# Two pairs of gate tiles by seven block products, softmax's small operations in pairs, one subtraction on GpSimd, four outputs begun early

## The chip, the cores and the metric

The kernel runs on one core of one Trainium2 chip. The metric is the time of one execution on the device, in microseconds; lower is better. Each kernel is run several times and the median is compared.

## The reference, cut to what matters

One decoder layer in float32, with 1024 tokens and 1024 channels:

```python
h = rms_norm(x, norm_mix_pre)
q_d, k_d, v_d, u_p, q_m, gate_logits = split(h @ w_in)
# branch A: 8 heads, two softmax maps per head, 64 wide; values 128 wide
s = q @ k * 64 ** -0.5 - slope[head] * distance          # causal
p = softmax(s)
a = (p[0] - lam * p[1]) @ v
y_attn = (rms_norm(a, subln_g) * 0.8) @ w_attn_branch
y_pool, y_mem = ...                                       # branches B and C
gates = sigmoid(gate_logits)                              # three times 1024 channels
mix = gates[0] * y_attn + gates[1] * y_pool + gates[2] * y_mem
x = x + rms_norm(mix @ w_out, norm_mix_post)
... gated feed-forward layer with a convolution over three tokens
```

The change touches the first gate's logits (gates[0], 1024 channels), the attention's softmax, the norm of each head and the product with `w_attn_branch`.

## The kernel before, in words

Activations lie transposed, channels on the 128 partitions and tokens along the free axis. A "tile" of a projection is 128 output channels by 1024 tokens. Every float32 operand is split into a high half (a copy to a type with fewer bits, on ScalarE) and a low half (the difference, on VectorE), and each product is three matmuls: high by high, high by low, low by high (`mm3`, lines 103 to 105; `split`, lines 89 and 90). The gate logits are thus, tile by tile, either

- `gate(dt)` (line 1116): one tile, 2 token halves x 8 channel blocks x 3 matmuls of 128x512 = 48 matmuls. It is a generator of eight steps of 6 matmuls each, so that it can be dealt out between other work; or
- `channels(c0)` with `seven` (line 198): two tiles at once as a 2 x 2 block product by seven products of half size (a Strassen-Winograd form with sums of weights and of inputs), each product 4 blocks x 3 matmuls, together 84 matmuls. The sums of inputs (`hops`, T1 to T4) exist only in the stage ahead of the attention.

The stages around the change are, in order:

1. The channel stage (to about 606 us of the span). `channels` makes the gates of the two other branches, keys of heads 0 and 1, all queries (four pairs of tiles, stored to `q_d` by SP) and gate tiles 0 and 1.
2. The attention, 8 heads of 4 blocks of 2 x 128 queries (606 to 882 us). Per block: `scores` (line 1161 on TensorE, the bias and the running maximum in one VectorE instruction at 1165, the exponent with its sum on ScalarE at 1170), `combine` for each of the two query tiles (reciprocal 1181, a small product 1182, and the difference of the two maps 1184, all on VectorE), `turn_weights` (transposes, line 1200, then a split), `weigh_values` (line 1217, then copy, square, and the square's two halves, 1219 to 1226), and `head_norm` (a product with ones, line 1235, whose row goes to `ss_d` by GpSimd's DMA queue). The first tile's `combine` is called right after the second tile's scores; the second tile's one block later, ahead of the turn. Between these stages `weave` deals out fillers: projections of the next head's keys (heads 1 to 6), and the gate tiles that `GATES` names: tiles 2 and 3 in head 0, tile 4 in head 7.
3. After the last weighing: `turn_sums(1)`, `load_norms(1)`, then gate tiles 5, 6 and 7, the norms of heads 4 to 7 (`head_norms(1)`, VectorE, written to `r_d` by SP and read back as a row for all partitions), and per head a load of its output `a`, of its row `rb`, a product (line 1384) and a split into `ath` and `atl`.
4. The merge: `merge_heads(dt, g)` adds the product of `w_attn_branch` with the heads of group g (0 to 3, 4 to 7) for output tile dt, `merge(dt)` applies the gate, adds the other two branches and splits. Outputs 0 and 1 are begun with group 0 ahead of heads 4 to 7.

Each engine takes its instructions in an order fixed when the program is built: a planner goes by the order of the program, lets an engine that would stand idle take a later instruction that is ready, and `issue_after(x)` holds the instructions of its block behind x on x's engine. SP and GpSimd issue the DMAs, in such an order too. Tile pools of one side are stacked: a pool that is closed hands its place to the next one, and a new tile waits for the last users of the tiles that lay there. The attention's pools are, in order, `qkp` (queries and keys), `att` and `vp` (values); `atp` (`ath`, `atl`) and `sub` (`a`, `rb`) take their place.

Of the kernel before, what the change touches and what calls it, by code (L numbers as in the profile page):

```python
# [8 lines left out]
F32 = mybir.dt.float32  # L9
# [3 lines left out]
ALU = mybir.AluOpType  # L13
# [28 lines left out]
def kernel(  # L42
# [818 lines left out]
    with tc.tile_pool(name="gp", reuse_waits="tile", bufs=2, side="right") as gp_:  # L861
# [163 lines left out]

        ss = gp_.tile([P, 4, H4, P], F32, tag="g", name="ss", bufs=3)
# [4 lines left out]
        ready = {2: wsplit(chunk(w_in, C_G + 2 * P), [P, KT, P])}  # L1031
        with tc.issue_after(ready[2][2].ins):
            late[0]()
# [10 lines left out]
    bias = ap_.tile([P, 1152], F32, name="bias", bufs=1)  # L1044
# [5 lines left out]
    def head_bias(h):  # L1050
        biases[h] = ap_.tile([P, 1152], F32, tag="hbias", name="hbias", bufs=2)
        nc.scalar.activation(out=biases[h], in_=bias, func=AF.Copy, scale=2.0 ** -(h + 1))
# [87 lines left out]
    def scores(h, b, u):  # L1140
# [9 lines left out]
        sm = small.tile([P, 1], F32, tag="sm", name="sm")  # L1150
# [5 lines left out]
        for c in range(2):  # L1156
            pss = bank2(name="pss2")
            for i in range(parts):
                keys = ks[c][:, i * m:(i + 1) * m]
                for j in range(2):  # L1160
                    last["scores"] = nc.tensor.matmul(pss[:, i * H:i * H + m], q[:, j, c, ts], keys,  # L1161
                                                      start=(j == 0), stop=(j == 1))
            z = ap_.tile([P, S], F32, tag="z%d" % c, name="z", bufs=3 - c)
# [7 lines left out]
                                 bias=mx[:, c:c + 1], accum_out=sm if c else sums[:, h, t:t + 1])  # L1171
        exps[h, b, u] = z2, mx, sm
# [3 lines left out]
    def combine(h, b, u):  # L1176

        z2, mx, sm = exps.pop((h, b, u))
        t = 2 * b + u
        n = (t + 1) * P  # L1180
        nc.vector.reciprocal(out=mx[:, 1:2], in_=sm)
        nc.vector.scalar_tensor_tensor(
            out=mx[:, 0:1], in0=mx[:, 1:2], scalar=sums[:, h, t:t + 1], in1=nlam, op0=ALU.mult, op1=ALU.mult)
        last["combine"] = nc.vector.scalar_tensor_tensor(
            out=z2[0][:, 0:n], in0=z2[1][:, 0:n], scalar=mx[:, 0:1], in1=z2[0][:, 0:n],
            op0=ALU.mult, op1=ALU.add)
        zts[h, b, u] = z2[0]
# [17 lines left out]
    def weigh_values(h, b):  # L1205
# [10 lines left out]
        for n, ((k, qs, w, ws), i, j) in enumerate(terms):  # L1216
            nc.tensor.matmul(po[:, qs], (vh, vl)[i][:, k, :], w[j][:, ws], start=(n == 0), stop=(n == len(terms) - 1))  # L1217
# [580 lines left out]
```

## Time and profile before

| | before |
|---|---|
| time, median of 3 runs | 1728.39 us (1727.39 to 1730.04) |
| profiled execution, span from first to last instruction | 1727.6 us |
| mean granted clock of TensorE | 0.999 |
| busy: ScalarE | 886.6 us (51%) |
| busy: GpSimd | 45.0 us (3%) |
| DMA traffic | 294.41 MB, mean 170 GB/s |

The page gives no time of the profiled execution other than its span. Busy time of an engine is the union of its instructions. PE is TensorE, PEld its weight loads (beside the matmuls), DVE VectorE, ACT ScalarE, POOL GpSimd, SP the queue that issues most DMAs. The ends of matmuls are modelled: each 128x512 matmul is shown as about 390 ns although the next one starts after some 226 ns, so the starts are to be read. A window's row gives, behind its length, the busy time and the number of instructions of each engine.

### The profile page before, as it was taken

To read this page: it belongs to the slowest core of one execution; us is meant where nothing else is said; L and a number is where in the kernel's file an instruction comes from. 1 tells how busy PE (TensorE), PEld (TensorE's weight loads), DVE (VectorE), ACT (ScalarE), POOL (GpSimd) and SP (SyncE) were. 2 spreads that over 40 slices of the span, in tenths; PEclk is the share of its full clock that TensorE was granted. 3 is DMA by queue.
4 is the path that set the end of the run, shared out by engine and by line. 5 is a ranking of instruction groups with operands and counts; after the bars stand their busy time and mean duration, and the time that the engine had idled before them with its cause. 6 is when DMAs were issued, how large, how long until landed. Compare 5 with 4: busy or idle time off the path is not lost.

```text
span 1727.6 us, 22400 instructions
## 1 busy us (share of the span) xinstructions
PE 1712.8 (99%) x8106; PEld 1421.4 (82%) x8106; DVE 1241.3 (72%) x2047; ACT 886.6 (51%) x1577; POOL 45.0 (3%) x103
## 2 busy tenths in 40 slices
PE   9999999999999999999999999999999999999998
PEld 7888888887888888888888888888888888888886
DVE  6765875666665578888866555848888888878466
ACT  5434544434544467777754344645555555543453
POOL 0000000000000011111110000000000000000000
PEclk9999999999999999999999999999999999999999
DMA  8873544444874686665556571572333423583344
GB/s 273 317 281 114 163 150 133 166 147 143 266 237 159 201 231 170 176 182 152 145 187 239 176 230 50 171 225 92 124 112 107 122 85 98 190 299 106 107 149 142
DMA packets 232803, 294.41 MB, mean 170 GB/s; under 512 B 15865, under 2 KB 161526, under 8 KB 230006
## 3 DMA queue, kind: packets, MB, share of 16 engines
q1 hardware_dynamic: 229158, 285.61, 51.8%
q0 software_dynamic: 3520, 7.38, 1.2%
q8 instruction: 64, 1.05, 0.3%
q14 instruction: 45, 0.37, 0.1%
q10 hardware_dynamic: 16, 0.00, 0.0%
HBM read 201.10 MB, written 85.56 MB: 166 GB/s over the span
## 4 chain that ended last, share of the span: by engine, by line
PE 91%; DVE 5%; DMA 2%; ACT 1%; issue 1%; SPq 0%; DVEq 0%; ACTq 0%
PE pa L103 8%; PE pa L104 8%; PE pa L105 8%; PE pb L103 5%; PE pb L104 5%; PE pb L105 5%; PE pss L1161 3%; PE poa L1217 2%; PE pd L103 2%; PE pd L105 2%; PE pd L104 2%; PE pe L105 2%; PE pe L104 2%; PE pe L103 2%; PE pout L103 2%; PE pout L105 2%
## 5 line engine op out<-in xcount | busy, mean ns | idle before, releaser
L89 ACT ACTIVATE wpage<-s 128x512 fp32r<-128x512 f32 x136 | 85.3, 627 | 108.2 <-DVE s L188 35.3
L90 DVE TENSOR_TENSOR wpage<-s,wpage 128x512 fp32r<-128x512 f32 x136 | 92.8, 688 | 43.2 <-ACT wpage L89 43.2
L1565 DVE SCALAR_TENSOR_TENSOR cvt<-gv,cols,cvt 128x1023 f32<-128x1023 f32 x88 | 112.5, 1278 | 15.6 <-ACT cvt L1561 14.9
L1165 DVE CUSTOM_DVE_ANT_0 z<-pss,hbias 128x256 f32<-128x256 f32 (+7 forms) x128 | 94.5, 752 | 26.0 <-PE pss L1161 24.8
L1170 ACT ACTIVATE z<-z,mx 128x256 f32<-128x256 f32 (+7 forms) x128 | 98.8, 773 | 20.8 <-DVE mx L1165 20.7
L103 PE MATMUL pa<-T,wpage 128*128 128x512 f32 x264 | 102.8, 389 | 0.0
L105 PE MATMUL pa<-T,wpage 128*128 128x512 f32 x264 | 102.7, 389 | 0.0
L104 PE MATMUL pa<-T,wpage 128*128 128x512 f32 x264 | 102.7, 389 | 0.0
L1161 PE MATMUL pss<-ks,q 128*128 128x512 f32 (+5 forms) x384 | 86.6, 349 | 1.4 <-DVE mx L1165 1.4
L89 ACT ACTIVATE page<-blk 128x1024 fp32r<-128x1024 f32 (+1 forms) x42 | 41.4, 989 | 85.7 <-PE pe L104 50.6
L90 DVE TENSOR_TENSOR page<-blk,page 128x1024 fp32r<-128x1024 f32 (+1 forms) x42 | 47.5, 1130 | 38.1 <-ACT page L89 38.1
L1161 PEld LDWEIGHTS pss<-ks,q 128*128 128x128 f32 x384 | 62.9, 189 | 11.1 <-DVE mx L1165 6.2
L103 PE MATMUL pd<-page 128*128 128x512 f32 x176 | 68.7, 390 | 0.0
L104 PE MATMUL pd<-page 128*128 128x512 f32 x176 | 68.5, 389 | 0.0
L105 PE MATMUL pd<-page 128*128 128x512 f32 x176 | 68.3, 389 | 0.0
L103 PE MATMUL pa<-hT,wpage 128*128 128x512 f32 x168 | 65.5, 390 | 0.1
L105 PE MATMUL pa<-hT,wpage 128*128 128x512 f32 x168 | 65.4, 389 | 0.0
L104 PE MATMUL pa<-hT,wpage 128*128 128x512 f32 x168 | 65.4, 389 | 0.0
L1217 PEld LDWEIGHTS poa<-aT,v 128*128 128x128 f32 x480 | 60.7, 190 | 3.0 <-ACT srow L1237 1.4
L1217 PE MATMUL poa<-aT,v 128*128 128x256 f32 (+1 forms) x480 | 62.5, 280 | 0.0
L103 PEld LDWEIGHTS pa<-T,wpage 128*128 128x128 f32 x264 | 49.6, 188 | 10.7 <-DVE gv L250 0.3
L104 PEld LDWEIGHTS pa<-T,wpage 128*128 128x128 f32 x264 | 49.6, 188 | 10.2
(429 smaller groups left out, 4965.7 us busy)
## 6 DMA issues: line engine op xcount, KB each, us to landing
q<-q_d SPq DMA_DIRECT2D x64, 256.0 KB, 5.1
wd<-in_w_down_dram SPq DMA_DIRECT2D x22, 512.0 KB, 5.0
tw_d<-wd SPq DMA_DIRECT2D x11, 1024.0 KB
rawv<-in_w_up_dram SPq DMA_DIRECT2D x22, 512.0 KB, 5.8
rawu<-in_w_up_dram SPq DMA_DIRECT2D x22, 512.0 KB, 4.1
ff_d<-cvt SPq DMA_DIRECT2D x22, 512.0 KB, 5.4
blk<-ff_d SPq DMA_DIRECT2D x20, 512.0 KB, 7.9
br<-tw_d SPq DMA_DIRECT2D x20, 512.0 KB, 5.0
```

The source lines that it names most:

```text
L89: copy = nc.scalar.activation(out=hi, in_=src, func=AF.Copy)
L90: nc.vector.tensor_tensor(out=lo, in0=src, in1=hi.bitcast(F32), op=ALU.subtract)
L103: nc.tensor.matmul(o, ah, bh, start=first, stop=False, skip_group_check=onto)
L104: nc.tensor.matmul(o, ah, bl, start=False, stop=False, skip_group_check=onto)
L105: return nc.tensor.matmul(o, al, bh, start=False, stop=last, skip_group_check=onto)
L1161: last["scores"] = nc.tensor.matmul(pss[:, i * H:i * H + m], q[:, j, c, ts], keys, start=(j == 0), stop=(j == 1))
L1165: nc.vector.tensor_tensor_reduce(out=halves(z[:, 0:n]), in0=pss.rearrange("p (a m) -> p a m", a=2)[:, 0:parts, 0:m], in1=halves(biases[h][ ...
L1170: nc.scalar.activation(out=z[:, 0:n], in_=z[:, 0:n], func=AF.Exp, scale=-1.0, bias=mx[:, c:c + 1], accum_out=sm if c else sums[:, h, t:t + 1])
L1217: nc.tensor.matmul(po[:, qs], (vh, vl)[i][:, k, :], w[j][:, ws], start=(n == 0), stop=(n == len(terms) - 1))
L1565: nc.vector.scalar_tensor_tensor(out=cv[:, sh:], in0=u[:, 0:S - sh], scalar=w, in1=cv[:, sh:], op0=ALU.mult, op1=ALU.add)
```

## The change

- Gate tiles 2 to 5 are made in the channel stage, as two pairs by `channels`, and stored by SP. Head 0 keeps one gate tile as filler (now tile 6), head 7 gets the first four of tile 7's eight steps, and the other four come after the last block: the first of them free, three held behind the last weighing (`ends["poa"]`). Tile 4 is no longer in head 7, tiles 5 to 7 no longer after the attention.
- `combine` takes both query tiles of a block at once: one reciprocal and one small product over two columns, then the two differences. It is called one block later, ahead of the turn. The second map's tiles get three buffers instead of two.
- The low half of the squares is subtracted on GpSimd instead of VectorE, and the store of the head's output on GpSimd's queue stands behind it.
- The attention's pools change order (`vp`, `att`, `qkp`); the bias shares the buffers of the heads' biases, each made from the one before.
- The loads of heads 0 to 3 (`load_head`) come first after the attention, ahead of the norms' loads; their products and splits (`normed_head`) follow. The stores of the sums go by ScalarE's queue.
- The merge takes outputs in pairs, with weights in blocks of 4 x 256 columns; two pairs, outputs 0 to 3, are begun with heads 0 to 3, in all eight PSUM banks.

```diff
+        for dt in (2, 4):
+            g = channels(C_G + dt * P)
+            nc.sync.dma_start(out=gate_d[dt:dt + 2].rearrange("e p s -> p e s"), in_=g)
...
-        ready = {2: wsplit(chunk(w_in, C_G + 2 * P), [P, KT, P])}
+        ready = {6: wsplit(chunk(w_in, C_G + 6 * P), [P, KT, P])}
...
+    vpool = cstack.enter_context(tc.tile_pool(name="vp", reuse_waits="tile", bufs=2, side="right"))
+    ap_ = cstack.enter_context(tc.tile_pool(name="att", reuse_waits="tile", bufs=3, side="right"))
     qkp = cstack.enter_context(tc.tile_pool(name="qkp", reuse_waits="tile", bufs=1, side="right"))
-    ap_ = cstack.enter_context(tc.tile_pool(name="att", reuse_waits="tile", bufs=3, side="right"))
-    vpool = cstack.enter_context(tc.tile_pool(name="vp", reuse_waits="tile", bufs=2, side="right"))
...
-            z = ap_.tile([P, S], F32, tag="z%d" % c, name="z", bufs=3 - c)
+            z = ap_.tile([P, S], F32, tag="z%d" % c, name="z", bufs=3)
...
+    def combine(h, b):
+
+        both, sm = exps.pop((h, b))
+        nc.vector.reciprocal(out=sm, in_=sm)
         nc.vector.scalar_tensor_tensor(
-            out=mx[:, 0:1], in0=mx[:, 1:2], scalar=sums[:, h, t:t + 1], in1=nlam, op0=ALU.mult, op1=ALU.mult)
...
+            out=sm, in0=sm, scalar=nlam, in1=sums[:, h, 2 * b:2 * b + 2], op0=ALU.mult, op1=ALU.mult)
+        for u, (z0, z1) in enumerate(both):
+            n = (2 * b + u + 1) * P
+            last["combine"] = nc.vector.scalar_tensor_tensor(
+                out=z0[:, 0:n], in0=z1[:, 0:n], scalar=sm[:, u:u + 1], in1=z0[:, 0:n],
+                op0=ALU.mult, op1=ALU.add)
+            zts[h, b, u] = z0
...
-        nc.gpsimd.dma_start(out=ao_d[h][:, bs], in_=ao)
-
...
-        ends["square"] = nc.vector.tensor_tensor(out=sqs[1], in0=sq, in1=sqs[0].bitcast(F32), op=ALU.subtract)
+        ends["square"] = nc.gpsimd.tensor_tensor(out=sqs[1], in0=sq, in1=sqs[0].bitcast(F32), op=ALU.subtract)
+        nc.gpsimd.dma_start(out=ao_d[h][:, bs], in_=ao)
...
-        nc.sync.dma_start(out=sum_d[g * HG:(g + 1) * HG].rearrange("h (t p) -> (h t) p", p=P), in_=row)
+        nc.scalar.dma_start(out=sum_d[g * HG:(g + 1) * HG].rearrange("h (t p) -> (h t) p", p=P), in_=row)
...
-    GATES = ((2, 3), (), (), (), (), (), (), (4,))
...
-                    combine(*blocks[n - 1], 1)
+                    combine(*blocks[n - 1])
                     turn_weights(*blocks[n - 1])
                 stages.append(weights)
             stages.append(lambda h=h, b=b: scores(h, b, 1))
-            stages.append(lambda h=h, b=b: combine(h, b, 0))
...
+        if h == 0:
+            for n, step in enumerate(steps(first, 6)):
+                fillers.insert(min(2 * n, len(fillers)), step)
+        if h == NH - 1:
+            tail = steps(gate(7), 8)
+            fillers, tail = fillers + tail[:4], tail[4:]
...
-    def merge_heads(dt, g):
+    def merge_heads(d, g):
         if g == 0:
-            pys[dt] = wsplit(chunk(w_attn_branch, dt * P), [P, KT, P])[:2] + (bank(name="pya"), pbank(name="pya"))
...
+            both = ([bank2((P, 2, H), "pya") for _ in range(2)] if d % 2 == 0 else
+                    [(bank(name="pya"), pbank(name="pya")) for _ in range(2)])
+            pys[d] = [[b[:, 0, :], b[:, 1, :]] if d % 2 == 0 else list(b) for b in both]
+        wh, wl = mws.pop((d, g))
+        order = [(k, e, i) for k in range(H4) for e in range(2) for i in range(2)]
+        if d >= 2 and g == 1:
+            order = [(k, e, i) for e in range(2) for i in range(2) for k in range(H4)]
+        for k, e, i in order:
+            h, hs, es = g * HG + k, slice(i * H, (i + 1) * H), slice(e * P, (e + 1) * P)
+            mm3(pys[d][e][i], wh[:, k, es], wl[:, k, es], ath[h][:, hs], atl[h][:, hs], h == 0, h == NH - 1)
...
+        for h in range(HG):
+            load_head(h)
+        load_norms(1)
+        for n, step in enumerate(tail):
+            with tc.issue_after(ends["poa"].ins) if n else nullcontext():
+                step()
+        for h in range(HG):
+            normed_head(h)
+        merge_weights(1, 0)
+        with tc.issue_after(ends["square"].ins):
+            head_norms(1)
+        merge_heads(0, 0)
+        merge_weights(0, 1)
+        merge_heads(1, 0)
+        merge_weights(1, 1)
+        for h in range(HG, NH):
+            load_head(h)
+            normed_head(h)
```

More of the change, by code (lines that the diff above doesn't have):

```diff
@@ L1149, in scores @@
         mx = small.tile([P, 2], F32, tag="mx", name="mx")
-        sm = small.tile([P, 1], F32, tag="sm", name="sm")
+        if u == 0:
+            exps[h, b] = [], small.tile([P, 2], F32, tag="sm", name="sm")
+        both, sm = exps[h, b]
         z2 = []
@@ L1254, in load_norms @@
         for src, r in ((ss_d, 0), (sum_d, 3)):
[L1255 removed]
+            with tc.issue_after(marks["head"].ins) if g else nullcontext():
+                nc.sync.dma_start(out=st[:, r], in_=src[g * HG:(g + 1) * HG].rearrange("h (p f) -> p h f", f=8))
         hns[g] = st
@@ L1276 @@
     load_keys(0)
-    first = gate(2)
+    first = gate(6)
     head_bias(0)
@@ L1369, with load_head @@
                                 op0=ALU.mult)
-        for dt in range(5, KT):
-            for step in steps(gate(dt), 8):
-                step()
-        for h in range(NH):
-            if h == HG:
-                with tc.issue_after(ends["square"].ins):
-                    head_norms(1)
-                for dt in range(2):
-                    merge_heads(dt, 0)
+        heads = {}
+        def load_head(h):
             a = sub.tile([P, S], F32, tag="a", name="a")
```

69 lines of the change are left out of this document (30 added, 39 removed).

## The prediction

> **What bounds the kernel.** I read the page first (busy shares, granted clock), then busy time by windows cut at the stages around the change, then the waits of TensorE, then groups and timelines inside the attention.
>
> ```profile
> span 1727.6 us, 22400 instructions
> ...
> PE 1712.8 (99%) x8106; PEld 1421.4 (82%) x8106; DVE 1241.3 (72%) x2047; ACT 886.6 (51%) x1577; POOL 45.0 (3%) x103
> ```
>
> TensorE is busy for 99% of the span, so the question about every edit is what it does to TensorE's queue: fewer matmuls, or a hole in it. The windows are 40 us of the channel stage, head 0, head 4, head 7 up to its last scores, the last block's chain, the gate tiles after the attention, and the merge:
>
> ```profile
> 520.00:560.00 40.00, 40.00 (x179) 33.10 (x178) 22.80 (x32) 16.76 (x26) 0.00 (x0) 1.00 0.46 164
> ...
> 606.00:641.00 35.00, 34.24 (x186) 29.44 (x187) 25.81 (x66) 22.88 (x54) 4.46 (x8) 1.00 0.80 214
> ...
> 740.00:773.00 33.00, 32.62 (x203) 28.13 (x202) 28.97 (x76) 25.82 (x66) 4.33 (x9) 1.00 0.64 177
> ...
> 838.00:867.00 29.00, 27.83 (x168) 23.80 (x167) 24.13 (x63) 21.91 (x55) 4.30 (x8) 1.00 0.40 112
> 867.00:882.00 15.00, 15.00 (x97) 12.54 (x95) 10.16 (x18) 8.78 (x19) 2.12 (x4) 1.00 0.23 65
> 882.00:911.00 29.00, 29.00 (x129) 23.80 (x128) 16.78 (x29) 11.20 (x16) 3.78 (x7) 1.00 0.81 288
> 911.00:1000.00 89.00, 89.00 (x394) 73.68 (x394) 52.06 (x65) 37.20 (x50) 0.54 (x1) 1.00 0.63 209
> ```
>
> The columns are length, then busy us and count of PE, PEld, DVE, ACT, POOL, then clock, DMA share and GB/s. In the merge 394 matmuls fill 89.00 us: one 128x512 matmul costs 89.00/394 = 0.226 us of TensorE's queue, and the clock is full everywhere. Channel stage and merge have no hole; the heads have small ones, and in head 4 VectorE is busy 28.97 of 33 us, so it is the engine next in line. TensorE's waits between 600 and 940 us:
>
> ```profile
> PE pss L1161 <- DVE mx L1165: 1.4, 4, 0.5
> PE pta L1200 <- DVE z L1184: 1.3, 3, 0.6
> ...
> ```
>
> Together 2.7 us for VectorE in 340 us, none longer than 0.6. (A matmul's end is modelled later than the next one's start, so waits under some 0.2 us do not show.)
>
> **Step 1, the matmuls.** A gate tile alone takes 2 halves x 8 blocks x 3 = 48 matmuls of 512 columns, so tiles 2 to 5 take 192. As two pairs by seven products of 4 x 3 matmuls they take 2 x 84 = 168. 24 fewer: 24 x 0.226 = **-5.4 us**. The 168 go to the channel stage, where 179 matmuls fill 40 us already and VectorE is busy 22.80 of 40; that stage has another such pair of tiles every 19 us, with two 512 KB loads and a 1 MB store on SP's queue. I cost the move itself at nothing: the store of a pair waits on SP for the pair's last copy, ahead of the next pair's loads, just as the stores of the q channels do today, and TensorE shows no hole there.
>
> **Step 2, head 0.** It loses tile 3.
>
> ```profile
> L103 PE MATMUL pg<-hTh,wh 128*128 128x512 f32 x27 | 10.9, 403 | 0.6 <-ACT g L1130 0.6
> ```
>
> That is one of three like rows of this head: 81 gate matmuls, 18.3 us, fill it. Without 48 of them TensorE's work is 35.0 - 10.8 = 24.2 us. VectorE's is 25.8 us less what the change takes off it, which needs these rows (606 to 882 us):
>
> ```profile
> L1182 DVE SCALAR_TENSOR_TENSOR mx<-mx,sums,nlam 128x1 f32<-128x1 f32 x64 | 13.8, 215 | 4.8 <-ACT z L1170 3.7
> L1226 DVE TENSOR_TENSOR sq<-sq,sq 128x256 fp32r<-128x256 f32 x31 | 13.0, 420 | 2.4 <-ACT sq L1225 2.3
> ...
> L1181 DVE RECIPROCAL mx<-sm 128x1 f32<-128x1 f32 x64 | 10.0, 158 | 8.7 <-ACT z L1170 8.4
> ```
>
> One pair of small operations for two tiles instead of one each saves 4 x (0.215 + 0.158) = 1.5 us per head, the squares' low halves 4 x 0.42 = 1.7 us: 3.2 us per head. So VectorE comes to about 22.6 us, still under 24.2. The head shortens nearly by its matmuls; but with less filler its start, where scores, maximum, exponent and turn follow one another, lies bare. Between 0 and +2.0 us (the head has 0.76 us of holes today at twice the filler); I take **+0.5**.
>
> **Step 3, heads 1 to 6.** VectorE is 3.2 us lighter in some 33, and TensorE can win back at most the 2.7 us above. Against it: the first tile's combination, which today is ready early, now waits for the second tile's sum, so both run ahead of the turn. The last block shows the size:
>
> ```profile
> 870.70 1.15 DVE L1184 SCALAR_TENSOR_TENSOR z<-z,mx 128x896 f32<-128x896 f32 x1
> ...
> 872.02 1.28 DVE L1184 SCALAR_TENSOR_TENSOR z<-z,mx 128x1024 f32<-128x1024 f32 x1
> ```
>
> Where TensorE already waits for a combination (3 times) up to 1.15 us more can follow: +3.5. From -2.7 to +3.5; I take **-1.2**, nearer the relief, since the relief works at all 24 blocks and the lateness shows only where no other matmul is ready.
>
> **Step 4, head 7 and the last chain.** From the last scores to the last weighing the chain is maximum, exponent, combination, turn, split:
>
> ```profile
> 864.57 2.29 PE L1161 MATMUL pss<-ks,q 128*128 128x512 f32 x8
> ...
> 878.93 3.00 PE L1217 MATMUL poa<-aT,v 128*128 128x256 f32 x24
> ```
>
> TensorE is full in it only because gate matmuls fill it (groups, 867 to 882 us):
>
> ```profile
> L103 PE MATMUL pg<-hTh,wh 128*128 128x512 f32 x11 | 4.5, 409 | 0.0
> ```
>
> With its two like rows (11 and 10) these are 32 matmuls, 7.2 us, of tiles 4 and 5. After the change only tile 7 is left: of its eight steps of 6 matmuls four are woven into head 7, one is free and three are held behind the last weighing. If step four and the free one fall into the chain, 12 fill it and 20 x 0.226 = 4.5 us lie bare; if the weaving lets more steps slip here, nothing does. The chain itself hardly shortens: both combinations now follow the last sum. Between 0 and +4.5; I take **+2.5**, a little over the middle, because head 7 in front is full for only 27.83 of 29 us and will draw steps early.
>
> **Step 5, after the last weighing (T = 881.93).** Today TensorE is covered by gate tiles for 29 us. After: 18 held matmuls and the begun outputs' first halves, 2 x 48, together 114 x 0.226 = 25.8 us. Two chains must fit. The first is the second four heads' norms:
>
> ```profile
> 886.91 0.36 SPq L1255 DMA_DIRECT2D hn<-ss_d  x1
> 887.38 0.45 SPq L1381 DMA_DIRECT2D a<-ao_d  x1
> ...
> 895.51 0.37 SPq L1267 DMA_DIRECT2D r_d<-hn  x1
> ...
> 903.49 0.33 SPq L1383 DMA_DIRECT2D rb<-r_d  x1
> ```
>
> ```profile
> 893.64 1.28 DVE L1384 SCALAR_TENSOR_TENSOR a<-a,gs,rb 128x1024 f32<-128x1024 f32 x1 [0.40 <-DMA rb<-r_d]
> ...
> 896.05 1.23 DVE L90 TENSOR_TENSOR atl<-a,ath 128x1024 fp32r<-128x1024 f32 x1 [0.57 <-ACT ath L89]
> ...
> 908.92 1.28 DVE L1384 SCALAR_TENSOR_TENSOR a<-a,gs,rb 128x1024 f32<-128x1024 f32 x1 [2.05 <-DMA rb<-r_d]
> ```
>
> T to the issue of r_d is 13.6 us; today its reader follows 8.0 us later, behind eight loads of 512 KB that stand in the queue; from that reader's issue to the product 5.4 us, and the head is split 896.05 + 1.23 - 893.64 = 3.6 us after that. 13.6 + 5.4 + 3.6 = 22.6, plus a wait for r_d of 0 to 8.0: 22.6 to 30.6 against 25.8, so 0 to +4.8. GpSimd's subtraction lies in this chain too. The loads of the first four heads are moved ahead of the norms, so the queue should be empty by then; I take **+0.5**. The second chain, those first four heads, I take as hidden; its price is the last rival.
>
> **Sum.** -5.4 + 0.5 - 1.2 + 2.5 + 0.5 = -3.1. The profiled execution spans 1727.6 us, the runs' median is 1728.4; I add the 0.8 as what lies around the span. 1728.4 - 3.1 = **1725.3**. All steps at their best ends give -8.1, at their worst +9.4.
>
> **Rivals.** *Nothing lies bare.* Gate steps slip into the last chain, head 0 costs nothing, and most of the relief comes: -5.4 - 2.0 = 1721.0. For it: the filler is placed wherever TensorE would stand idle, as the full last chain shows. Against it: 20 matmuls are simply not there.
>
> *GpSimd hands back what VectorE saved.* No row shows a subtraction on GpSimd. The nearest are VectorE's own 0.42 us and GpSimd's
>
> ```profile
> L1047 POOL TENSOR_SCALAR_AFFINE_SELECT bias<-bias 128x1152 f32<-128x1152 f32 x1 | 1.6, 1612 | 0.0
> ```
>
> which is 1.40 ns per element, 0.36 us for 256, and 0.72 if two inputs take twice as long. If VectorE stands still while one runs, 4 per head give back 1.4 to 2.9 us of its 3.2, and step 3 is left with the late combination alone, about +1.5: -5.4 + 0.5 + 1.5 + 2.5 + 0.5 = -0.4, 1728.0. For it: the combinations read two tiles from SBUF just as the subtraction does. Against it: GpSimd's DMA issues run beside VectorE today and TensorE waits little. The Trainium skill says this outright: in "SBUF — State Buffer", section "SBUF: two separate sides", a VectorE instruction with two SBUF inputs and a GpSimd one that reads SBUF exclude each other, and the later one blocks for the whole instruction. By "GPSIMD Engine Reference", section 3.1, an addition of 2048 takes GpSimd 4.497 us, so I would estimate 0.56 us for 256. No run here shows either yet.
>
> *The first four heads come late.* TensorE reaches the first begun output 18 x 0.226 = 4.1 us after T. Today a head is ready 896.05 + 1.23 - 887.38 = 9.9 us after its load is issued, and that load goes out 5.5 us after T. If the new places in memory free the loads only at T, TensorE waits 9.9 - 4.1 = 5.8 us; if it stays as today, 11.3; loads issued before T - 5.8 = 876.1 us cost nothing. With the other terms: 1725.3 + 5.8 to 11.3 = 1731.1 to 1736.6; I name 1734. For it: four heads of 1 MB each must land, and GpSimd and the weights share the DMA engines. Against it: the pools change places, so that the loads should lie over keys and queries, which are free after the last scores (866.9).
>
> **Chances.** Forecast 0.45, nothing bare 0.27, GpSimd 0.15, heads late 0.13. A measurement of this kernel can tell about 0.2%, 3.5 us, from no change: below 1724.9 is faster, above 1731.9 slower. The forecast's own range is 1722.5 to 1728.5, with 0.20 of its 0.45 below 1724.9. Faster: 0.27 + 0.20 = 0.47; same: 0.25 + 0.15 = 0.40; slower: 0.13. The range 1719.5 to 1731.0 takes in the first three cases and the relief's far end, and leaves out the last one.
>
> **What would show it.** Right: 24 fewer matmuls; two more full 19 us blocks before the attention; head 0 shorter by about 10 us; a hole of 2 to 3 us between the last scores and the last weighing; none after it; fewer waits of line 1161 on VectorE. Wrong: longer combinations beside GpSimd's subtractions; TensorE waiting for a normed head of either four; a hole at the end of a head that names the combination.

## The result and the profile after

| | before | after |
|---|---|---|
| median of the runs made side by side | 1728.27 us | 1753.05 us (1750.77 to 1754.59) |
| ratio, 95% interval | | 1.0142 (1.0128 to 1.0157) |
| span of the profiled execution | 1727.6 us | 1752.6 us |

The change makes the kernel 24.8 us slower; the forecast was 3 us faster, with 1731.0 as the upper end of its range. These are the lines of the page of after that answer to those shown of before; the last is TensorE's granted clock in 40 slices.

```profile
span 1752.6 us, 22357 instructions
...
PE 1722.4 (98%) x8082; PEld 1419.8 (81%) x8082; DVE 1238.0 (71%) x1975; ACT 892.2 (51%) x1587; POOL 66.4 (4%) x127
...
PEclk9999999999999999999989999999999999999999
```

The 24 matmuls are gone (8106 to 8082), yet TensorE is busy for longer, and one slice has lost clock. The windows of after, cut at the same stages: channel stage, heads 0, 4 and 7, the last chain, the time up to the first begun output, the merge, the output projection (columns as in the prediction; the column behind POOL is the clock).

```profile
600.00:640.00 40.00, 40.00 (x178) 33.12 (x177) 16.33 (x25) 12.08 (x21) 2.74 (x3) 1.00 0.47 136
642.00:669.00 27.00, 26.02 (x146) 21.45 (x146) 20.64 (x53) 20.95 (x49) 4.68 (x7) 1.00 0.97 256
...
771.00:804.00 33.00, 32.90 (x203) 28.57 (x203) 26.15 (x71) 25.07 (x63) 7.38 (x12) 1.00 0.69 190
869.00:898.00 29.00, 27.41 (x170) 22.64 (x169) 23.41 (x56) 22.89 (x58) 7.35 (x12) 1.00 0.43 120
898.00:917.00 19.00, 14.84 (x79) 12.71 (x78) 11.56 (x17) 8.16 (x19) 2.87 (x5) 0.73 0.15 49
917.00:924.00 7.00, 4.85 (x21) 3.40 (x20) 0.00 (x0) 2.99 (x6) 2.43 (x4) 1.00 0.51 144
924.00:1017.00 93.00, 89.69 (x386) 71.79 (x387) 60.60 (x83) 35.56 (x46) 0.00 (x0) 1.00 0.70 232
1017.00:1115.00 98.00, 94.57 (x435) 78.07 (x434) 53.52 (x102) 40.03 (x77) 0.00 (x0) 0.98 0.40 123
```

The channel stage is as dense as it was: step 1 holds. The last chain is the worst stage: 79 matmuls in 19 us, at a mean clock of 0.73, where before there were 97 in 15. Behind it, places that were full have holes: the start of the merge, and the output projection, which before was this row:

```profile
998.00:1090.00 92.00, 92.00 (x432) 76.65 (x431) 51.34 (x98) 37.89 (x74) 0.00 (x0) 1.00 0.37 121
```

For a ledger I took, for each matmul, the time from its start to the start of the next, less the usual spacing of its form (0.2265 us for 512 columns, 0.119 for 256, 0.109 for 128, and so on for the scores' other lengths), and summed it by stage. It counts waits and half clock alike. After less before:

| stage | forecast | ledger |
|---|---|---|
| 24 matmuls fewer (step 1) | -5.4 | -5.4 |
| up to the first scores | 0 | -1.1 |
| heads 0 and 1 (step 2; head 1 is in step 3) | +0.5 | +5.4 |
| heads 2 to 6 (step 3) | -1.2 | +2.1 |
| head 7 and the last chain (step 4) | +2.5 | +1.7 + 8.1 |
| from the last weighing to the first begun output, and from there to the end of the merge (step 5) | +0.5 | +2.5 + 5.6 |
| output projection | 0 | +5.5 |

The sum is +24.4, against 25.0 between the spans. So nothing large happened at one place. The loss is spread over five, and at each of them TensorE had less cover than before, that is, fewer matmuls that depend on nothing and can be worked off while a chain of other engines is not ready. TensorE's longest waits from 600 to 1120 us of after (who waits, for whom; sum, times, longest):

```profile
PE pya L103 <- ACT ath L89: 2.9, 2, 1.6
PE pta L1206 <- DVE z L1190: 2.7, 4, 1.2
PE pout L103 <- ACT woh L89: 2.3, 1, 2.3
PE pya L104 <- DVE atl L90: 1.6, 3, 0.7
PE pn L1240 <- POOL sq L1230: 1.6, 5, 0.5
```

None is over 2.3 us. In the last chain they lie together (timeline of TensorE and VectorE, in brackets the wait ahead of the instruction and who ended it):

```profile
903.09 2.90 DVE L1190 SCALAR_TENSOR_TENSOR z<-z,sm 128x896 f32<-128x896 f32 x2
...
904.38 0.42 PE L1206 MATMUL pta<-ident,z 128*128 128x128 f32 x2 [0.80 <-DVE z L1190]
906.05 0.97 PE L1206 MATMUL pta<-ident,z 128*128 128x128 f32 x6 [1.24 <-DVE z L1190]
908.00 1.76 PE L1206 MATMUL pta<-ident,z 128*128 128x128 f32 x7 [0.99 <-DVE aT L90]
...
911.88 5.26 PE L1223 MATMUL poa<-aT,v 128*128 128x256 f32 x24
```

Both combinations stand behind the last sum, the gate matmuls that are not held behind the last weighing have been used up by then, and the 24 matmuls of the last weighing take 5.26 us instead of 3.00. The clock explains that:

```profile
904.00:908.00 4.00, 1.39 (x8) 0.90 (x8) 3.87 (x5) 1.11 (x3) 0.88 (x2) 0.84 0.09 33
908.00:912.00 4.00, 2.87 (x11) 2.18 (x12) 2.72 (x5) 1.35 (x3) 0.00 (x0) 0.50 0.00 0
912.00:916.00 4.00, 4.00 (x21) 4.00 (x20) 0.32 (x1) 0.37 (x1) 0.51 (x1) 0.50 0.02 4
```

TensorE worked for 1.39 of 4 us, and for the next 8 us it was granted half the clock.

### The profile page after: what moved, and what is told of

The parts are those of the page before. It is cut to its first block, busy times and chain, and to the rows that moved or that the text cites. A ratio compares the mean times of both kernels' runs of the same rounds, so it can differ in the third digit from the quotient of the medians.

```text
span 1752.6 us, 22357 instructions
## 1 busy us (share of the span) xinstructions
PE 1722.4 (98%) x8082; PEld 1419.8 (81%) x8082; DVE 1238.0 (71%) x1975; ACT 892.2 (51%) x1587; POOL 66.4 (4%) x127
## 5 line engine op out<-in xcount | busy, mean ns | idle before, releaser
L89 ACT ACTIVATE wpage<-s 128x512 fp32r<-128x512 f32 x144 | 90.3, 627 | 115.4 <-DVE s L188 50.0
L90 DVE TENSOR_TENSOR wpage<-s,wpage 128x512 fp32r<-128x512 f32 x144 | 98.1, 687 | 48.7 <-ACT wpage L89 48.7
L1600 DVE SCALAR_TENSOR_TENSOR cvt<-gv,cols,cvt 128x1023 f32<-128x1023 f32 x88 | 112.5, 1278 | 14.5 <-ACT cvt L1596 14.4
L103 PE MATMUL pa<-hT,wpage 128*128 128x512 f32 x192 | 74.8, 389 | 0.3 <-ACT wpage L89 0.3
L105 PE MATMUL pa<-hT,wpage 128*128 128x512 f32 x192 | 74.7, 389 | 0.0
L104 PE MATMUL pa<-hT,wpage 128*128 128x512 f32 x192 | 74.7, 389 | 0.0
```

The costliest lines, as they stand in the source:

```text
L89: copy = nc.scalar.activation(out=hi, in_=src, func=AF.Copy)
L90: nc.vector.tensor_tensor(out=lo, in0=src, in1=hi.bitcast(F32), op=ALU.subtract)
L103: nc.tensor.matmul(o, ah, bh, start=first, stop=False, skip_group_check=onto)
L104: nc.tensor.matmul(o, ah, bl, start=False, stop=False, skip_group_check=onto)
L105: return nc.tensor.matmul(o, al, bh, start=False, stop=last, skip_group_check=onto)
L1600: nc.vector.scalar_tensor_tensor(out=cv[:, sh:], in0=u[:, 0:S - sh], scalar=w, in1=cv[:, sh:], op0=ALU.mult, op1=ALU.add)
```

## The experiments

Two theories stood at first. **A:** TensorE has lost its cover in several places (head 0, last chain, start of the merge, output projection), and each costs on its own. **B:** GpSimd's subtraction and VectorE shut each other out, and the heads become longer. Runs that change after come first, then parts of the change put into before. All ratios are to before, run side by side; "under after" compares what each run is above its own before with the 24.8 us of after.

### One mending at a time, on after

**hole_filled:** 40 transposes of the identity, which nothing reads, behind the last block's turn.

```diff
     turn_weights(*blocks[-1])
+    dum = bank2((P, 8, P), "dum")
+    for j in range(40):
+        nc.tensor.transpose(dum[:, j % 8, :], ident, ident)
```

> The changed kernel with 40 dummy transposes (128x128, into a bank that nobody reads) behind the turn of the last block, and nothing else. Theory A (the loss comes from four places, one of them the hole before the last weighing, which also halves TensorE's clock): the hole keeps its length but the clock stays at 1.00, the last weighing's 24 matmuls take 2.9 us again instead of 5.3 and the transposes 0.1 us each; 2.5 to 3.5 us gained, about 1750. Theory B (GpSimd's subtraction locks VectorE out, and the heads are longer for it): nothing gained, the same as the changed kernel or up to 2 us more for the dummies.

1749.6 us, 1.0118 (1.0101 to 1.0135): 3.5 us under after, as expected, by work that computes nothing. From the window of the chain and its timeline:

```profile
898.00:917.00 19.00, 17.80 (x126) 15.38 (x125) 11.30 (x17) 9.07 (x21) 4.46 (x8) 1.00 0.17 57
```

```profile
910.54 3.00 PE L1223 MATMUL poa<-aT,v 128*128 128x256 f32 x24
```

The clock is 1.00 again, and the weighing is back at 3.00 us and starts 1.3 us earlier. The clock is a cost of its own, beside the hole.

**ones_apart** (ones and sums in a place that outlives the attention), **last_single** (outputs 6 and 7 one after the other, as before), **combine_early** (one combination per tile, the first before the second tile's sum, as before), **square_dve** (the square's low half back on VectorE), **free_tail** (tile 7's last three steps not held):

```diff
-    ones = ap_.tile([P, P], F32R, name="ones", bufs=1)
+    ones = keepp.tile([P, P], F32R, name="ones", bufs=1)
...
+        if d == 3:
+            for dt in (6, 7):
+                wh, wl, _ = wsplit(chunk(w_attn_branch, dt * P), [P, KT, P])
...
-                    combine(*blocks[n - 1])
+                    combine(*blocks[n - 1], 1)
...
+            stages.append(lambda h=h, b=b: combine(h, b, 0))
...
-        ends["square"] = nc.gpsimd.tensor_tensor(out=sqs[1], ...
+        ends["square"] = nc.vector.tensor_tensor(out=sqs[1], ...
...
-            with tc.issue_after(ends["poa"].ins) if n else nullcontext():
-                step()
+            step()
```

> The changed kernel with the matrix of ones and the sums in a small pool of their own, ahead of the attention's pools, so that no loaded head lies on them. Theory A (the row of head 1 stands on SP's queue until the last norm has read the ones, and the loads of heads 1 to 3 stand behind it): that row's load goes out ahead of the last weighing instead of 2.6 us after it, TensorE no longer waits for splits of heads 1 to 3; 2 to 5 us gained, 1748 to 1751. Theory B (GpSimd's lock): the loads may move, the time does not, within 1 us of 1753.

> The changed kernel with the last two outputs made one after the other (weights of all 1024 rows for one output, as before) instead of as a pair. Theory A (a pair leaves four gated halves, not two, to be finished when TensorE has reached the output projection, and the splits of its weights stand behind them on ScalarE): TensorE's waits for woh and wol at 1024 us (2.3 and 1.1 us) and the half clock after them go; 4 to 6 us gained, 1747 to 1749. Theory B (GpSimd's lock in the heads): no gain, within 1 us of 1753.

> The changed kernel with the combination of each query tile by itself and the first tile's called right after the second tile's scores, as before. Theory A (late combinations make the turn late, in heads 0 and 1 and at the ends of heads above all): the waits of line 1206 on 1190 shrink, and the last chain is about 1.2 us shorter with its half clock; 2 to 5 us gained, 1748 to 1751. Theory B (GpSimd's lock): four more small VectorE operations per head and the same subtractions: no gain, or up to 2 us slower.

> The changed kernel with the squares' low halves subtracted on VectorE again, and nothing else. Theory A (the lock exists but meets a combination only a few times; the subtraction on GpSimd mainly lengthens the wait of the norm's matmul by 0.3 us): between 1 us gained and 1 us lost, 1752 to 1754. Theory B (GpSimd's subtraction locks VectorE out and the heads are longer for it): 5 us or more gained, 1748 or less.

> The changed kernel with the three last steps of tile 7 (18 matmuls, 4.1 us) not held behind the last weighing. Theory A: the planner puts them into the hole before the last weighing, the clock does not fall, about 4 + 3 us gained there; but behind the last weighing 4.1 us of cover are gone and TensorE waits that much longer for the first head's split, which nothing hurries: net 2 to 4 us gained, about 1750. Theory B (GpSimd's lock): no change.

| run | median | ratio (95%) | under after (us) |
|---|---|---|---|
| ones_apart | 1751.76 | 1.0132 (1.0117 to 1.0147) | 1.3 |
| last_single | 1750.73 | 1.0130 (1.0115 to 1.0146) | 2.3 |
| combine_early | 1748.77 | 1.0120 (1.0105 to 1.0135) | 4.3 |
| square_dve | 1752.20 | 1.0142 (1.0127 to 1.0157) | 0.35 |
| free_tail | 1747.78 | 1.0114 (1.0098 to 1.0129) | 4.8 |

square_dve has the ratio of after: theory B falls as the explanation of the loss. combine_early came as expected, free_tail did better, last_single and ones_apart less. The intervals of these runs overlap that of after (1.0128 to 1.0157), free_tail's by a hair, so a single gain stands on what the trace shows at its place more than on the time. In ones_apart the load of head 1's row is issued at 909.66 us instead of 919.72, as expected, and the time hardly moves: that load was not what the heads waited for.

### The order of the heads, and all mendings together

**heads_first** is ones_apart with `normed_head(0..3)` written ahead of the tail's steps; **all_mended** is that with free_tail, last_single and combine_early.

> The kernel after, with the matrix of ones and the sums in a place of their own and the first four heads' normalisation written ahead of gate tile 7's last four steps instead of behind them, so that on ScalarE and VectorE these heads' splits stand ahead of the gate's last eviction. Theory (the heads are late because of the order of ScalarE's and VectorE's work, no longer because of their loads): the wait ahead of the first begun output goes from 2.7 us to under 0.7, and 2 to 4 us of the merge's lost 5.7 go with it: 1747 to 1750 us, 1.0105 to 1.0125 of before. Rival (the splits of a head cost more than TensorE's work on a head, so the lateness only moves from the first wait to the next ones, or the splits now delay the last chain): 1750.5 to 1753.

> The kernel after with all five mendings at once: ones in a place of their own, the heads' splits ahead of the gate's last steps, those steps not held behind the last weighing, the first combination of each pair early as before, and the last two outputs one by one. Theory A (the loss lies at separate places where TensorE has lost its cover): the gains add up, 4 us for the combinations, 5 for the steps set free, 2 for the last outputs and 3 to 6 for the heads' order: 1735 to 1740 us, and what is left over before is head 0's 5 us and the merge. Rival (each mending takes its cover from another place, so that they don't add up): 1743 to 1748.

heads_first: 1751.44, 1.0135 (1.0122 to 1.0148), as ones_apart; a miss. The planner still puts head 0's split behind the gate's last eviction. all_mended: 1741.62, 1.0073 (1.0060 to 1.0086): 10.9 us under after, clear of its interval, and between the two expectations. The gains of heads_first (1.1), free_tail, last_single and combine_early add up to 12.5 us, and by the ratios both come to 0.69%: within the noise they add, and what fell short were the single gains. The chain is mended (14.8 us from the last scores to the last weighing, where after has 16.8 and before 14.4), the start of the merge is not:

```profile
910.00:915.00 5.00, 2.25 (x8) 1.18 (x8) 1.88 (x2) 2.18 (x4) 2.29 (x4) 1.00 0.90 297
915.00:920.00 5.00, 5.00 (x16) 3.92 (x15) 2.96 (x3) 1.94 (x2) 0.00 (x0) 0.66 0.29 51
```

The same picture as in after's chain: 2.25 us of work in 5, then full work at 0.66 of the clock. Two runs on all_mended take up the two causes that this leaves, **products_ahead** (head h + 2's product on VectorE ahead of head h + 1's low half) and **clock_kept** (24 idle transposes in the wait for the first head):

```diff
+            with tc.issue_after(last["hp"].ins):
+                nc.vector.tensor_tensor(out=atl[h], in0=a, in1=ath[h].bitcast(F32), op=ALU.subtract)
+            if h + 2 < HG:
+                head_product(h + 2)
...
+        with tc.issue_after(ends["poa"].ins):
+            for j in range(24):
+                nc.tensor.transpose(dum[:, j % 8, :], ident, ident)
```

> all_mended with the first four heads' products on VectorE each moved ahead of the low half of an earlier head (product of head h + 2 ahead of the low half of head h + 1), so that the three operations of a head no longer stand in series with the next head's. Theory (behind the last weighing TensorE waits because product, split and low half of one head follow one another and the next head's product stands behind the low half): the heads come every 2.5 us instead of 3.5, and the merge loses 1.5 to 3 us less: 1738.5 to 1740. Rival (the merge's loss is the half clock that follows the wait ahead of the first begun output, not the pace of the heads): 1741 to 1742.5.

> all_mended with 24 transposes of the identity, which nothing reads, on TensorE between the last weighing and the first begun output, in the wait for the first normed head. They add work of 2.6 us in a wait of 2.9 us. Theory (after the wait TensorE is granted half the clock for some microseconds, and that is most of what the start of the merge loses): the clock stays at 1.00 there and 1 to 2 us come back: 1739.5 to 1740.5. Rival (the pace of the heads sets the time, and full clock only makes TensorE wait longer for the next head): 1741.5 to 1743.

1740.80, 1.0073 (1.0058 to 1.0089), and 1741.37, 1.0081 (1.0067 to 1.0095): neither changes the time, though clock_kept's clock is 1.00 from 910 to 920. The half clock comes later there:

```profile
940.00:945.00 5.00, 4.78 (x12) 3.37 (x13) 5.00 (x6) 4.30 (x5) 0.00 (x0) 0.66 0.80 265
```

What both runs leave alone is the chain of the second four heads' norms. In all_mended the last weighing ends at 909.2 us:

```profile
917.06 0.37 SPq L1265 DMA_DIRECT2D hn<-ss_d  x1
...
928.53 0.37 SPq L1277 DMA_DIRECT2D r_d<-hn  x1
...
939.23 0.74 PE L103 MATMUL pya<-ath,wh 128*128 128x512 f32 x2 [0.85 <-ACT ath L89]
```

The row is stored 19.3 us after the last weighing; before it was 13.6. **norms_free** and **norms_free_clock** (with the 24 transposes) take the wait for it away: heads 4 to 7 are scaled by the rows of heads 0 to 3, which changes the output, while their own norms are still computed and stored.

```diff
-            marks["head"] = nc.sync.dma_start(out=rb, in_=r_d[h:h + 1, :].partition_broadcast(P))
+            marks["head"] = nc.sync.dma_start(out=rb, in_=r_d[h % HG:h % HG + 1, :].partition_broadcast(P))
```

> all_mended, but the last four heads are normalised by the rows of the first four (so the output is not the reference's): their own norms are still computed and stored, and nobody waits for them. Theory (in all_mended the first-begun outputs' second halves wait for the second four heads' norms, which stand on VectorE behind the first four heads, 19 us after the last weighing instead of the 13.6 of before): the waits at the fifth head go, 1.4 us and what follows them: 1739 to 1740.5 against 1741.6. Rival (the fifth head is late because VectorE and ScalarE are still with the first four): no change, 1741 to 1742.5.

> The same with the 24 transposes of clock_kept in the wait for the first head (same departure from the reference). Theory (clock_kept brought nothing only because the second four heads' norms end at the same time whatever TensorE does before, so that TensorE gave back at the fifth head what the full clock had won): here the two gains add, 3 to 4 us under all_mended: 1737 to 1739. Rival: 1740 to 1742, as clock_kept.

1739.85, 1.0070 (1.0053 to 1.0087), and 1738.30, 1.0060 (1.0045 to 1.0075). Both times are in the range of the theory, but the intervals overlap that of all_mended, and the traces bear out only half of it. These are the starts of some matmuls in microseconds, counted from the end of the last weighing:

| first matmul of | all_mended | products_ahead | clock_kept | norms_free | norms_free_clock |
|---|---|---|---|---|---|
| the second head | 8.87 | 9.11 | 7.60 | 8.99 | 7.62 |
| the fourth head | 14.69 | 14.60 | 14.71 | 14.66 | 14.69 |
| the second pair of outputs | 18.00 | 17.35 | 18.02 | 18.00 | 18.01 |
| the sixth head | 33.48 | 33.43 | 35.76 | 31.73 | 31.74 |
| 25th of the output projection | 102.43 | 102.10 | 104.39 | 100.37 | 100.37 |
| last of the output projection | 192.60 | 191.64 | 194.45 | 190.83 | 188.99 |

The full clock puts clock_kept and norms_free_clock 1.3 us ahead at the second head, and at the fourth they are level with the others: TensorE waited for the heads instead. So the rival of clock_kept is right, and not the theory that the gain was lost at the fifth head. (There clock_kept loses another 2.3 us, to a wait of 1.5 us instead of 0.85 and the half clock behind it; the execution profiled was the slowest of its four.) products_ahead is 0.65 us ahead when the second pair of outputs begins, and 0.05 at the sixth head: here the second four heads' norms do take the gain back. Without the wait for them norms_free is 1.75 us ahead of all_mended at the sixth head and stays so. norms_free_clock is level with norms_free up to the output projection, and the 1.8 us that it leads by arise there, where TensorE has no wait for `wol` (1.1 us in norms_free). That its time fell into the expected range was luck. A run with products_ahead and norms_free together was not made.

### Parts of the change, on before

**one_pair** makes tiles 2 and 3 as a pair in the channel stage and leaves all else as before: tile 4 in head 0, 5 in head 7, 6 and 7 behind the attention. **two_pairs** does so with tiles 2 to 5, as the change does: 6 in head 0, 7 in head 7, none behind. **head0_two** has one pair and keeps two tiles (4 and 5) in head 0; 6 is in head 7 and 7 alone behind.

```diff
+        for dt in (2,):
+            g = channels(C_G + dt * P)
+            nc.sync.dma_start(out=gate_d[dt:dt + 2].rearrange("e p s -> p e s"), in_=g)
...
-    GATES = ((2, 3), (), (), (), (), (), (), (4,))
+    GATES = ((4,), (), (), (), (), (), (), (5,))
```

> The kernel before with only gate tiles 2 and 3 made as one pair in the channel stage; tile 4 fills head 0, tile 5 head 7, tiles 6 and 7 follow the attention; combination, square, pools, loads and merge as before. Theory A (the saving of 12 matmuls is real, and is lost only where cover is missing; here one gate tile of cover is missing in head 0 and one after the attention, where 9 us were spare): 12 x 0.226 = 2.7 us gained less up to 2 in head 0: 1725 to 1728. Theory B (GpSimd's lock is what cost): 2.7 us gained in full, 1725.5.

> The kernel before with gate tiles 2 to 5 as two pairs in the channel stage, tile 6 in head 0, tile 7 in head 7, no gate tile after the attention; combination, square, pools, loads and merge as before. Theory A (cover is what counts): 5.4 us fewer matmuls, but the last chain lies bare (about 4 us, and 3 more by the clock) and after the last weighing nothing is ready until the first head is loaded, which in the kernel before took 15 us from there, then heads come every 3.6 us: 15 to 22 us lost, 1738 to 1748. Theory B (GpSimd's lock is what cost): 5.4 us gained, 1723.

> The kernel before with tiles 2 and 3 as one pair of block products, as in the run one_pair, but with two tiles (4 and 5) woven into head 0 as before, tile 6 in head 7 and tile 7 alone behind the attention: the missing tile is taken from behind the last weighing and not from head 0. Theory A: heads 0 and 1 come back to what they were (4 to 5 us better than in one_pair), while behind the last weighing 11 us less stand before the normed heads, which come late by 3 to 8 us: 1731 to 1739 us. If head 0's filler was all that one_pair lost, and the heads after the last weighing are in time: 1724 to 1727. Rival (the pair in the channel stage itself costs what it saves): 1733 to 1735 with no new wait behind the last weighing.

one_pair 1734.56, 1.0039 (1.0024 to 1.0054): a miss, 12 matmuls fewer and 6.8 us slower. two_pairs 1755.58, 1.0159 (1.0142 to 1.0176), past the 1738 to 1748 expected: the moved tiles alone cost about as much as the whole change. head0_two 1739.04, 1.0061 (1.0049 to 1.0073), the far end of what was expected. The starts of heads 0 and 2 (first scores) in before, one_pair and head0_two:

```profile
605.32 0.56 PE L1161 MATMUL pss<-ks,q 128*128 128x128 f32 x4
...
674.10 0.56 PE L1161 MATMUL pss<-ks,q 128*128 128x128 f32 x4
```

```profile
624.60 0.56 PE L1165 MATMUL pss<-ks,q 128*128 128x128 f32 x4
...
686.97 0.56 PE L1165 MATMUL pss<-ks,q 128*128 128x128 f32 x4
```

```profile
622.63 0.56 PE L1165 MATMUL pss<-ks,q 128*128 128x128 f32 x4
...
691.68 0.56 PE L1165 MATMUL pss<-ks,q 128*128 128x128 f32 x4
```

Heads 0 and 1 take 68.8 us in before and 69.1 in head0_two, with the same 84 gate matmuls. one_pair takes 62.4 with 48 fewer, which are worth 48 x 0.226 = 10.9 us: 62.4 is 4.5 more than 68.8 - 10.9 = 57.9. So head 0's filler was hiding 4.5 us, and in head0_two they are hidden again. By the ledger the rest of one_pair's loss lies mostly in head 7 (1.2 us) and between the last weighing and the end of the merge (2.9). The pair itself costs nothing where it is made: the first scores come 19.28 us later than in before, and its 84 matmuls are worth 84 x 0.2265 = 19.0. In head0_two the tile is missing behind the last weighing:

```profile
PE pya L103 <- ACT ath L89: 7.1, 1, 7.1
```

That is head0_two's first begun output, 7.1 us late; by the ledger 13.0 us are lost between the last weighing and the end of the merge. The tile hides more there than in head 0.

**square_alone** is before with only the squares' low halves on GpSimd, **small_alone** has softmax's small operations for two tiles as well (with the bias's buffers that this needs).

> The kernel before with the squares' low halves on GpSimd and nothing else changed: 1.7 us of VectorE's work per head moved to another engine. Theory A (VectorE's relief brings nothing, and small_alone's loss came from the late combinations): 1727.5 to 1729.5. Theory B (GpSimd's subtraction hinders VectorE, or makes the norms late): 1730 to 1734. Step 3 of the prediction, as far as it rests on VectorE's relief: 1725 to 1727.

> The kernel before with only softmax's small operations for two tiles at once (with the bias tiles' places that this needs) and the squares' low halves on GpSimd: no tile is moved, the merge is as before. Theory A: with the cover of before in place the late combinations cost 1 to 4 us, above all behind the last scores, where up to 1.15 us of chain comes on top, and VectorE's 3.2 us per head bring nothing: 1728 to 1732 us. Rival (VectorE's relief is worth what step 3 of the prediction said): 1725.5 to 1727. Theory B (GpSimd's subtraction costs VectorE what it saves): 1728, with combinations longer by 0.5 us where both start together.

1730.28, 1.0014 (1.0005 to 1.0023), and 1733.82, 1.0032 (1.0020 to 1.0044). In small_alone VectorE is busy for 16 us less than before (1225.2 us), and the kernel is 6.1 us slower, past the 1728 to 1732 expected. square_alone is 2.3 us slower, at the near end of what theory B gave (GpSimd's subtraction hinders VectorE or makes the norms late), so on before theory B holds to this small size; TensorE has a new wait of 0.5 us for GpSimd's square. The profiled span, 1727.7, hides the loss, since this execution reaches the first scores earlier than that of before (605.32 us), in a stage that the edit does not touch:

```profile
603.42 0.56 PE L1161 MATMUL pss<-ks,q 128*128 128x128 f32 x4
```

From there to the end it is 2.0 us longer. By the ledger 2.1 us are in heads 1, 3 and 5 and 0.7 behind the last weighing, less 0.7 in head 7; what waits for what there was not followed up. The rest of small_alone's loss, 3.8 us, comes with the paired combination and its buffers, which were not tried apart.

## Why the prediction was wrong

**Step 1** was right in its count and in the stage: 24 fewer, no hole in the channel stage. "I cost the move itself at nothing" was said of that stage, and there it held (19.28 us for a pair worth 19.0). What failed is what the moved matmuls had been hiding at the places that they left: steps 2, 4 and 5 looked for it and sized it too small. All of one_pair's and two_pairs' losses come from it, since these two runs move tiles and do nothing else.

**Step 2** failed in size. "Between 0 and +2.0 us" was taken from the idle time of head 0 alone and from its sums of work; TensorE's 24.2 us against VectorE's 22.6 said that TensorE would still be the bound. The head is a chain of small steps, and what the filler hid there cost 4.5 us in one_pair and 5.4 in the ledger. In head 0 alone it was 1.6, inside the range; 3.8 lie in head 1, which the prediction did not look at: waits of 0.3 to 0.7 us at scores, turns and norms, none of which stands out.

**Step 3**: VectorE's relief, -2.7 at best, never showed: square_alone and small_alone relieve VectorE and are slower. The lateness of the combinations was real: 4.3 us in combine_early. By the ledger 1.5 of it is in heads 1 to 6, inside the step's +3.5, 1.4 in head 7 and 1.9 in the last chain.

**Step 4** had the right hole in the right place, as a wait for line 1190 behind the last sums, and 12 matmuls in it. It priced a hole by its length, "20 x 0.226 = 4.5 us", and left out the clock: TensorE worked for 1.39 us of 904 to 908, and was then granted 0.50 up to the end of the chain. hole_filled, which keeps the clock, brought 3.5 us back. The ledger has 8.1 us, past the end of the step's range.

**Step 5** failed in its two main numbers. Of the first four heads it said "I take as hidden", since their loads would be early. Head 0's were (issued at 883.3 and 883.7 us); those of heads 1 to 3 were complete only with issues from 919.72 to 921.55, 2.6 us and more behind the last weighing. Yet ones_apart, which issues head 1's row 10 us earlier, gained only 1.3 us: the work behind the loads was late too. The splits on ScalarE stand behind the gate's last eviction, and VectorE works off product, split and low half head by head:

```profile
911.04 1.28 DVE L1396 SCALAR_TENSOR_TENSOR a<-a,gs,rb 128x1024 f32<-128x1024 f32 x1
...
922.43 0.60 ACT L1134 ACTIVATE g<-pg 128x512 f32<-128x512 f32 x1 [2.37 <-PE pg L105]
922.92 1.05 ACT L89 ACTIVATE ath<-a 128x1024 fp32r<-128x1024 f32 x1
...
924.02 0.73 PE L103 MATMUL pya<-ath,wh 128*128 128x512 f32 x2 [1.63 <-ACT ath L89]
...
939.56 0.37 SPq L1273 DMA_DIRECT2D r_d<-hn  x1
```

Head 0's product is done at 912.3 us, its split starts at 922.92. And "T to the issue of r_d is 13.6 us" was carried over as if fixed; here it is 939.56 - 917.14 = 22.4 us. Of the 8.8 us more, 5.3 arise between the load of the sums (`hn`, issued at 925.69 us; in before at 886.91) and `r_d`, because the norms' small operations now stand on VectorE behind the four heads that were put first; the other 3.6 lie ahead of that load, which waits for the sums to be stored. The wait that the third rival named came (1.6 us where it said 5.8 to 11.3), and a second one at the fifth head.

**Not costed at all** was the merge in pairs at its end. The last four gated halves come at once, and `w_out`'s splits stand behind them on ScalarE. TensorE's timeline at the output projection:

```profile
1024.58 0.50 PE L103 MATMUL pout<-woh,mixh 128*128 128x512 f32 x1 [2.29 <-ACT woh L89]
1026.22 0.80 PE L104 MATMUL pout<-wol,mixh 128*128 128x512 f32 x1 [1.14 <-DVE wol L90]
```

The ledger has 5.5 us there. That the pairs alone cause it is not shown: last_single's ledger has 2.8 less there than after's, but ones_apart, free_tail and hole_filled, which leave the merge as it is, have 1.4 to 1.8 less too, and all_mended, with the last outputs one by one, still has 3.7.

**The GpSimd rival** was wrong as the cause of the loss: square_dve changed nothing, though on before the subtraction alone cost 2.3 us. Its price was right, 0.75 us against the 0.72 reckoned; it seldom met a combination. About 0.8 us of the prediction's base was off too: what lies around the span is 2.0 us in after's own profiled execution (1754.59 against 1752.6), not 0.8; this has no effect on the difference.

Of the ledger, heads 2 to 6 (+2.1) and head 7 (+1.7) had no run of their own; the late combinations explain 1.5 and 1.4 of it (combine_early's ledger), and the rest stays open, as does most of the loss in the output projection. No version tried beats before.

## What to carry to other kernels

Work that an engine does beside a chain of waits is worth more than its own time: before moving it, list what it hides, and price a hole with what the clock does after it. Mending one wait on a path of several shows only up to the next chain, so follow a gain by the starts of the same matmuls in both traces: a time inside the expected range does not show that it came for the expected reason. Relief of an engine can be worth no more than the others wait for it (here some 2.7 us), however many microseconds it is.

## What the hardware showed that was not expected

TensorE's clock was halved without a long stop. In after it worked for 1.39 us between 904 and 908 and had 0.50 from 908 to 916; in all_mended it worked for 2.25 us between 910 and 915 and had 0.66 from 915 to 920, when it was busy without a gap. The Trainium skill, "TensorE: Matmul & The Clock Gate", Part 1, speaks of an idle window of about 3.4 us, after which the clock is at half. The half rate agrees with these rows. An empty stretch of that length was not needed: the longest wait ahead of these two drops was 1.24 us in after, and 1.41 in all_mended.

A subtraction on GpSimd (0.75 us) and a combination on VectorE that start together hinder one (timeline of after):

```profile
696.42 1.57 DVE L1190 SCALAR_TENSOR_TENSOR z<-z,sm 128x768 f32<-128x768 f32 x1
...
696.42 0.75 POOL L1230 TENSOR_TENSOR sq<-sq,sq 128x256 fp32r<-128x256 f32 x1
```

The combination took 1.57 us instead of the 1.01 of before, 0.56 more. The Trainium skill, "SBUF — State Buffer", section "SBUF: two separate sides", says that the later one stands still for the whole instruction, which would be 0.75. Three subtractions that started inside a combination took 1.00 to 1.20 us instead of some 0.75. Of the 64 combinations here 4 were longer, each by 0.55 or 0.56 us; one is the last chain's second (1.83 us instead of 1.28).
